# Sample rows' new states formed along the gate and up tiles of the second feed-forward block, readout taken from the old state

## The chip, the core and the metric

One core of a Trainium2 chip runs one launch of the kernel. The metric is the device time of a launch in microseconds (us). Five engines work side by side, each with its own queue in order: TensorE (PE for matmuls, PEld for weight loads), VectorE (DVE), ScalarE (ACT), GpSimd (POOL) and SyncE (SP), which issues the transfers. "L772" is line 772 of the kernel before.

## The reference, cut to what matters

A decoder layer for 512 prompt rows and 8 sample rows (one new token for each of 8 sequences, with its stored state): a half-step SwiGLU block, a mixer of causal pooling and a state-space scan side by side, a second half-step SwiGLU block, and a last norm.

```python
h = h + 0.5 * swiglu(rms_norm(h, ffn1_norm), ...)
h = h + mixer(rms_norm(h, mix_norm), ...)
h = h + 0.5 * swiglu(rms_norm(h, ffn2_norm), ...)   # swiglu: (silu(x @ wg) * (x @ wu)) @ wd
return rms_norm(h, final_norm)
```

For a sample row, head by head, the scan is one step. With the old state h0 (64 x 128 for a head), the head's input x, its step dt, decay = exp(dt * A), and rows B and C of 128 numbers that 8 heads of a group share:

```
new state = decay * h0 + (dt * x) B        (an output, new_ssm_sample)
y         = new state . C + d_skip * x
```

y then goes through the gate with silu(z), a norm by group, and the output projection. The new state itself is needed by nothing else in the launch.

## The kernel before

Activations lie with features on the 128 partitions and the 520 rows (512 prompt, 8 sample, in two halves of 260) along the free axis. Each f32 product is made of three matmuls (`mm3`, L115 to L118): high part of the weights by high and low part of the activations, and low part of the weights by the high part. `split` (L101) makes the parts: ScalarE casts a weight tile to its high part (L106), VectorE subtracts to get the low part (L107).

The feed-forward blocks (`Ffn`) go over 22 tiles of the inner width in chunks of 8, 8 and 6. `rest` (L307) calls `step(f)` for each tile (L329): seven products of 12 matmuls each, copies of partial sums from PSUM (L284), then `gates` (L288: VectorE sums, a Silu on ScalarE in L292) and `close` (L295: the cast of the gated tile L299 and its low part L300). The weights of a tile (`load`, L245) come by two transfers of 512 KB into one of two raw buffers (L249, L250). From them VectorE forms sums (L256 to L258), and ScalarE and VectorE split four tiles: "whi_6a" is the high part of the first weights of tile 6, "shi_6c" and "shi_6d" those of its sums, "whi_6b" the rest. After each chunk, `down` (L339) multiplies the gated tiles with the down weights and adds them to h (L356 to L363); the last chunk does it by halves (`down_by_half`, L378). `scales` (L302) forms the rows' inverse norm (nx[3]) and a second tile rn, which is -0.5 times it (L305), and which the down epilogues L356 and L408 multiply by.

The mixer is written as two plans of stages (CONV_PLAN L38, GATE_PLAN L42): b, x, p and z are the input projections with their convolution or pooling, A and B the two parts of a chunk of the prompt's scan, G and H the gate and norm of a group, o, g and h the output projection, and s2 handles two sample units. A scan part loads a broadcast of decays by SyncE (ab, L796), forms exponentials on ScalarE and products on VectorE (L813, L818, L822), and TensorE multiplies (L831 to L838).

A sample unit is a sequence b and a group g of four 128-row blocks, 16 in all (`sample`, L760). It loads B's and C's rows, broadcast over the partitions (bcb, L764), and the state (h0, 256 KB, L767). For each of four blocks ScalarE makes B times dt*x (L771), VectorE forms decay * h0 plus that, in place (L772); the state is stored (L774), and VectorE multiplies it with C and sums along the row into ysm (L776). `gate` (L877) adds ysm to the sample columns (L884), multiplies with the silu of z (L886), and `gate_out` squares (L895), sums and normalises. The rows B and C of the samples are transposed and sent through a scratch in DRAM by `sample_bc` (L748).

A scheduler places the instructions: it runs through a timeline of its own, with estimated costs, takes on each engine the earliest traced instruction that it holds ready (those in a high-priority block first), and the resulting order of each engine's queue is fixed. `keep_in_program_order` puts an instruction behind the one traced last before it on the same engine. `issue_after(i)` puts a block's instructions that are on i's engine behind i. Tiles with the same tag share a number of buffers; an instruction that writes a reused buffer waits until the earlier tile's readers are done.

## Time and profile before

| what | us |
|---|---|
| three runs | 1028.15, 1032.51, 1027.37 |
| median | 1028.15 |
| profiled execution, its own time | 1030.91 |
| its span | 1029.1 |
| first feed-forward block and start | 0 to about 375 |
| mixer with output projection | about 375 to 633 |
| second feed-forward block to the end | about 633 to 1029.1 |

The span is the time from the first to the last instruction in the profile. An engine is busy while an instruction of its own executes; instructions of one engine overlap a little at their ends, so the distance between the starts of equal neighbours is less than one's duration. In a row of a group stand line, engine, operation, output and input tiles, shape and count, then the busy time and the mean of one, then the idle time in front of them and what ended it. A row of waits reads: who waited for whom, us in total, times, longest. A row of a timeline has start and duration. A row of a stretch has its bounds, its length, the busy time of PE, PEld, DVE, ACT and POOL with counts, the granted clock, the share in which the DMA engines were busy, and GB/s. A row of transfers ends with the median us from issue to landing.

### The profile page before, as it was taken

The page shows a single profiled execution, that of the slowest core. Times are in us where ns is not written, and L with a number is a line of the kernel's source. Part 1 is how long each engine was busy: PE and PEld are TensorE (multiplying, and loading weights), DVE is VectorE, ACT ScalarE, POOL GpSimd, SP SyncE. Part 2 cuts the span into 40 slices and gives each one's busy share as a digit, 9 for nine tenths or more (in the row PEclk, how much of TensorE's full clock was granted, in tenths as well). Part 3 has the DMA queues.
Part 4 walks back from the last instruction along what each step waited for, and adds up shares of the span by engine and source line. Part 5 has one row for each costly group of instructions (what it writes and reads, how often), then busy time and mean ns, then how long its engine had stood idle before and what let it go on. Part 6 is the DMA issues. An engine that isn't in the chain of part 4 may idle for free.

```text
span 1029.1 us, 19313 instructions
## 1 busy us (share of the span) xinstructions
PE 981.7 (95%) x7848; PEld 956.6 (93%) x7848; DVE 807.3 (78%) x1403; ACT 526.4 (51%) x884; POOL 57.0 (6%) x109
## 2 busy tenths in 40 slices
PE   7999999999999999997698999999999999999994
PEld 6999999999999999996598999899999999999994
DVE  7999557995578788689989877999954799557866
ACT  7566314663145555775486525656631566315552
POOL 0000000000000000337201000000000000000000
PEclk9999999999999999999899999999999999999997
DMA  5333223232232143355354222222323323232203
GB/s 186 111 124 123 83 87 119 83 124 82 88 118 93 55 138 116 126 173 183 110 174 145 94 103 82 69 96 91 115 83 103 103 88 119 82 103 104 93 32 83
DMA packets 45352, 110.25 MB, mean 107 GB/s; under 512 B 5896, under 2 KB 17096, under 8 KB 45264
## 3 DMA queue, kind: packets, MB, share of 16 engines
q1 hardware_dynamic: 45264, 109.03, 31.4%
q8 instruction: 61, 1.00, 0.4%
q14 instruction: 27, 0.22, 0.1%
HBM read 101.67 MB, written 7.34 MB: 106 GB/s over the span
## 4 chain that ended last, share of the span: by engine, by line
PE 42%; DVE 7%; ACT 4%; DMA 2%; issue 1%; POOL 1%; DVEq 0%; ACTq 0%; SPq 0%
PE A L116 4%; PE A L117 4%; PE A L118 4%; PE dn L118 3%; PE dn L116 3%; PE dn L117 3%; PE BE L116 3%; PE BE L118 3%; PE BE L117 3%; PE wo L116 2%; PE wo L118 2%; PE wo L117 2%; PE P L228 1%; PE dh L116 1%; DMA bcb<-scr_bc 1%
## 5 line engine op out<-in xcount | busy, mean ns | idle before, releaser
L356 DVE TENSOR_TENSOR td<-dn,rn 128x520 f32<-128x520 f32 x40 | 27.9, 699 | 112.5 <-PE dn L118 112.5
L116 PE MATMUL dn<-g,whi_1d 128*128 128x260 f32 x352 | 99.3, 283 | 1.7 <-ACT whi_1d L106 1.5
L117 PE MATMUL dn<-g,whi_1d 128*128 128x260 f32 x352 | 99.2, 282 | 0.0
L118 PE MATMUL dn<-g,wlo_1d 128*128 128x260 f32 x352 | 99.1, 283 | 0.0
L116 PE MATMUL dn<-g,whi_2d 128*128 128x260 f32 x256 | 72.5, 283 | 1.6 <-ACT whi_2d L106 1.6
L117 PE MATMUL dn<-g,whi_2d 128*128 128x260 f32 x256 | 72.3, 282 | 0.0
L118 PE MATMUL dn<-g,wlo_2d 128*128 128x260 f32 x256 | 72.1, 283 | 0.0
L116 PEld LDWEIGHTS dn<-g,whi_1d 128*128 128x128 f32 x352 | 66.1, 188 | 2.4 <-ACT whi_1d L106 2.0
L284 ACT COPY ac<-A 128x260 f32<-128x260 f32 x123 | 46.0, 375 | 41.3 <-PE A L118 39.7
L117 PEld LDWEIGHTS dn<-g,whi_1d 128*128 128x128 f32 x352 | 66.2, 188 | 0.0
L118 PEld LDWEIGHTS dn<-g,wlo_1d 128*128 128x128 f32 x352 | 66.1, 188 | 0.0
L106 ACT CAST whi_1d<-raw_1d 128x1024 fp32r<-128x1024 f32 (+1 forms) x24 | 23.4, 980 | 70.6 <-PE dn L117 62.2
L228 PE MATMUL P<-xg_f,raw 128*128 128x260 f32 x192 | 46.2, 398 | 5.3 <-DMA raw<-in_w1gu 5.2
L106 ACT CAST whi_2d<-raw_2d 128x1024 fp32r<-128x1024 f32 (+1 forms) x18 | 18.5, 1027 | 63.6 <-PE dn L117 59.2
L116 PEld LDWEIGHTS dn<-g,whi_2d 128*128 128x128 f32 x256 | 48.3, 189 | 2.0 <-ACT whi_2d L106 2.0
L256 DVE TENSOR_TENSOR s<-raw 128x1024 f32<-128x1024 f32 x41 | 49.9, 1217 | 0.0
L117 PEld LDWEIGHTS dn<-g,whi_2d 128*128 128x128 f32 x256 | 48.2, 188 | 0.0
L228 PEld LDWEIGHTS P<-xg_f,raw 128*128 128x128 f32 x192 | 37.5, 199 | 11.5 <-ACT xg_f L178 5.2
L118 PEld LDWEIGHTS dn<-g,wlo_2d 128*128 128x128 f32 x256 | 48.1, 188 | 0.0
L116 PE MATMUL wo<-catg,whi_wo 128*128 128x260 f32 x128 | 37.4, 292 | 0.2 <-DVE h L871 0.2
L116 PE MATMUL inz<-xh_mx,whi_inz 128*128 128x260 f32 x128 | 37.4, 292 | 0.0
L118 PE MATMUL inz<-xh_mx,wlo_inz 128*128 128x260 f32 x128 | 36.9, 288 | 0.0
(1334 smaller groups left out, 3920.3 us busy)
## 6 DMA issues: line engine op xcount, KB each, us to landing
raw<-in_w2gu SPq DMA_DIRECT2D x44, 512.0 KB, 3.7
raw<-in_w1gu SPq DMA_DIRECT2D x42, 512.0 KB, 4.4
raw_1d<-in_w1d SPq DMA_DIRECT2D x16, 512.0 KB, 3.7
raw_2d<-in_w2d SPq DMA_DIRECT2D x16, 512.0 KB, 4.4
raw_wo<-in_w_out SPq DMA_DIRECT2D x12, 512.0 KB, 4.6
h<-in_state_ssm SPq DMA_DIRECT2D x16, 256.0 KB, 4.8
ab<-scr_acs SPq DMA_DIRECT2D x8, 512.0 KB, 5.2
out_nss<-h SPq DMA_DIRECT2D x16, 256.0 KB, 3.3
```

What stands on the lines that cost most here:

```text
L106: nc.scalar.copy(h, src)
L116: nc.tensor.matmul(ps, whi, xhi, start=start, stop=False, **kw)
L117: nc.tensor.matmul(ps, whi, xlo, start=False, stop=False, **kw)
L118: nc.tensor.matmul(ps, wlo, xhi, start=False, stop=stop, **kw)
L228: nc.tensor.matmul(self.banks[f, u][b][:, :HB], ws(self.raw[f][:, u], j + 4 * q), xg[:, slot[q]], start=j == q == 0, stop=j == 3 and q == ...
L256: nc.vector.tensor_tensor(out=s1, in0=diag, in1=up0, op=ALU.add)
L284: nc.scalar.copy(keep, out[:, :HB])
L356: nc.vector.tensor_tensor(out=t, in0=banks[d][:, :, :HB], in1=self.rn.rearrange("p (b t) -> p b t", b=2), op=ALU.mult)
```

## The change

- `sample` loads only C's row and the old state, with buffers for three and four units, and VectorE multiplies the old state with C. The result goes to ysm, the product itself to a tile that nobody reads.
- `sample_bc` also forms, for each sample and group, the sum over B times C, by a small VectorE product and a matmul with ones (sbc). `sample_y`, called in `gate`, makes ysm * decay + (dt * x) * sbc, three VectorE operations for a group.
- `new_states` is a generator that `step` of the second block advances once for each tile from tile 3 on. Its first call loads the first unit; each later call loads the next unit (B's row and the state again) and forms the present one: for each of four blocks ScalarE makes B times dt*x and the scaled state, a transfer on POOL's queue adds the first onto the second in SBUF, and another stores it. Loads and scalings are kept in program order. Two buffers each.
- decay and dt*x (sdec, sxdt) move to a pool that lives on.
- The tile rn goes; the down epilogues multiply by -0.5 and nx[3] in one operation.
- `gate_out` squares whole rows into X, which is no longer needed, where it had squared halves.
- The samples' block under `issue_after` becomes plain.

```diff
@@ -199,6 +199,7 @@
 
         def __init__(self, nx, i, wx, gp, direct):
             self.nx, self.i, self.wx, self.gp, self.direct = nx, i, wx, gp, direct
+            self.states = None
             self.w, self.A, self.BE, self.ac, self.g, self.tg, self.raw, self.banks, self.behind = ({} for _ in range(9))
 
         def plain_load(self, f, j=None):
@@ -301,8 +302,6 @@
 
         def scales(self):
             rstds(self.nx, f"f{self.i}")
-            self.rn = self.wx.tile([P, NT], F32, tag="rn", bufs=1, name=f"rn{self.i}")
-            nc.vector.tensor_scalar(out=self.rn, in0=self.nx[3], scalar1=-0.5, scalar2=None, op0=ALU.mult)
 
         def rest(self, before, last_chunk):
             lo = 0
@@ -327,6 +326,8 @@
                 lo = hi
 
         def step(self, f):
+            if self.states is not None and f > 2:
+                next(self.states, None)
             if f not in self.A:
                 self.product(f, 1)
             if f - 1 not in self.g and f > self.direct:
@@ -353,8 +354,9 @@
             def done(d):
                 t = self.wx.tile([P, 2, HB], F32, tag="tg", bufs=2, name=f"td{self.i}_{d}_{c}")
                 hd = h[:, d].rearrange("p (b t) -> p b t", b=2)
-                nc.vector.tensor_tensor(out=t, in0=banks[d][:, :, :HB], in1=self.rn.rearrange("p (b t) -> p b t", b=2),
-                                        op=ALU.mult)
+                nc.vector.scalar_tensor_tensor(out=t, in0=banks[d][:, :, :HB], scalar=-0.5,
+                                               in1=self.nx[3].rearrange("p (b t) -> p b t", b=2), op0=ALU.mult,
+                                               op1=ALU.mult)
                 if after is None:
                     nc.vector.tensor_tensor(out=hd, in0=t, in1=hd, op=ALU.add)
                     return
@@ -405,7 +407,8 @@
             def done(d, b):
                 hs = HALVES[b]
                 t = self.wx.tile([P, 2, HB], F32, tag="tg", bufs=2, name=f"th{self.i}_{d}{b}")[:, 0]
-                nc.vector.tensor_tensor(out=t, in0=banks[d, b][:, :HB], in1=self.rn[:, hs], op=ALU.mult)
+                nc.vector.scalar_tensor_tensor(out=t, in0=banks[d, b][:, :HB], scalar=-0.5, in1=self.nx[3][:, hs],
+                                               op0=ALU.mult, op1=ALU.mult)
                 nc.vector.tensor_tensor(out=h[:, d, hs], in0=t, in1=h[:, d, hs], op=ALU.add)
                 after(d, b, hs)
 
@@ -491,6 +494,8 @@
     f2["xg"].release()
     xa[0].release()
     g2 = f2["ffn"].gp = pool("g2", "left")
+    f2["st"] = pool("st2", "left")
+    f2["ffn"].states = f2["states"](f2["st"])
     with tc.high_priority():
         f2["ffn"].scales()
         f2["ffn"].behind[2] = f2["ffn"].plain_out(0)
@@ -536,13 +541,14 @@
                 nc.sync.dma_start(out=outs["y"][:, q, t], in_=hg[:, q, t])
 
     f2["ffn"].rest(before2, after2)
-    for p in (ps[0], g2, f2["hg"], f2["wx"]):
+    for p in (ps[0], f2["st"], g2, f2["hg"], f2["wx"]):
         p.release()
 
 
 def mixer(tc, ins, outs, e):
     nc = tc.nc
     cst, act, wp, tmp, dr, pool = (e[x] for x in ("cst", "act", "wp", "tmp", "dr", "pool"))
+    ones = e["ones"]
     bank, load_unit, mm3, ws, v, rstd, rstds, vec, h, nx2, raw_tile, open_f2, fin, fill = (
         e[x] for x in ("bank", "load_unit", "mm3", "ws", "v", "rstd", "rstds", "vec", "h", "nx2", "raw_tile",
                        "open_f2", "fin", "fill"))
@@ -602,7 +608,7 @@
             if not k:
                 nc.tensor.matmul(dtb[b][:NH, :HB], w48[:, k, :NH], xl[:, k, hs], start=False, stop=False)
     rstds(nx2[0], "mx")
-    dv = mp.tile([48, NT], F32, tag="h0", bufs=2, name="dv")
+    dv = mp.tile([48, NT], F32, tag="h0", bufs=4, name="dv")
     for b, hs in enumerate(HALVES):
         nc.vector.tensor_tensor(out=dv[:, hs], in0=dtb[b][:48, :HB], in1=r[:48, hs], op=ALU.mult)
     tok = mp.tile([P, 2, NC + 1, NH], F32, tag="tok", name="tok")
@@ -705,7 +711,7 @@
         first = slice(PAST, PAST + w - 1)
         sx = slice(SAMPLE_P + PAST, LP, 16)
         nc.gpsimd.tensor_tensor(out=cur[:, first], in0=cur[:, first], in1=rcnt[:, : w - 1], op=ALU.mult)
-        held["pool"] = nc.gpsimd.tensor_tensor(out=cur[:, first], in0=cur[:, first], in1=U[:, first], op=ALU.subtract)
+        nc.gpsimd.tensor_tensor(out=cur[:, first], in0=cur[:, first], in1=U[:, first], op=ALU.subtract)
         nc.gpsimd.tensor_copy(npp[:, g], U[:, SEQ : SEQ + PAST])
         nc.gpsimd.tensor_copy(spool[:, g], us[:, :, 1:16])
 
@@ -730,10 +736,15 @@
 
 
     sdt = mp.tile([P, NX, NS], F32, tag="sdt", name="sdt")
-    sdec = mp.tile([P, NX, NS], F32, tag="sdec", name="sdec")
-    sxdt = mp.tile([P, NX, NS], F32, tag="sxdt", name="sxdt")
+    sdec = cst.tile([P, NX, NS], F32, tag="sdec", name="sdec")
+    sxdt = cst.tile([P, NX, NS], F32, tag="sxdt", name="sxdt")
     ysm = mp.tile([P, NX, NS], F32, tag="ysm", name="ysm")
+    sbc = mp.tile([P, 2, NS], F32, tag="sbc", name="sbc")
+    junk = act.tile([P, NT], F32, tag="acc", name="junk")[:, :P]
     scr_bc = dr.tile([NS, 512], F32, name="scr_bc")
+
+    def rows_bc(b, a, g):
+        return scr_bc.rearrange("b (a g n) -> b a g n", a=2, g=2)[b, a, g].unsqueeze(0).to_broadcast([P, P])
 
     def sample_decay():
         for j in range(2):
@@ -749,32 +760,60 @@
         bcs = bank("bcs")
         for j in range(4):
             nc.tensor.transpose(bcs[:NS, j * P : (j + 1) * P], BC[:, j, SEQ:NT], ident)
-        bct = mp.tile([NS, 512], F32, tag="ho", bufs=2, name="bct")
+        bct = mp.tile([NS, 512], F32, tag="h0", bufs=4, name="bct")
         nc.scalar.copy(bct, bcs[:NS, :])
         nc.sync.dma_start(out=scr_bc, in_=bct)
+        dots = bank("dots")[:, : 2 * NS]
+        nc.vector.tensor_tensor(out=sbc, in0=BC[:, 0:2, SEQ:NT], in1=BC[:, 2:4, SEQ:NT], op=ALU.mult)
+        nc.tensor.matmul(dots, ones, sbc.rearrange("p g b -> p (g b)"), start=True, stop=True)
+        nc.scalar.copy(sbc, dots.rearrange("p (g b) -> p g b", g=2))
 
     def sample_x(g):
         gs = slice(4 * g, 4 * g + 4)
         nc.vector.tensor_tensor(out=sxdt[:, gs], in0=sdt[:, gs], in1=X[:, gs, SEQ:NT], op=ALU.mult)
 
+
     def sample(b, g):
+        cb = tmp.tile([P, HB], F32, tag="ta", name=f"cb{b}{g}")[:, :P]
+        nc.sync.dma_start(out=cb, in_=rows_bc(b, 1, g))
+        h0 = mp.tile([P, 4, P], F32, tag="h0", bufs=4, name=f"h0_{b}{g}")
+        nc.sync.dma_start(out=h0, in_=ins["state_ssm"][:, b, 4 * g : 4 * g + 4])
+        for q in range(4):
+            nc.vector.scalar_tensor_tensor(out=junk, in0=h0[:, q], scalar=1.0, in1=cb, op0=ALU.mult, op1=ALU.mult,
+                                           accum_out=ysm[:, 4 * g + q, b : b + 1])
+
+    def sample_y(g):
         gs = slice(4 * g, 4 * g + 4)
-        shp = [P, 4, P]
-        bcb = mp.tile([P, 2, P], F32, tag="bcb", bufs=2, name=f"bcb{b}{g}")
-        nc.sync.dma_start(out=bcb, in_=scr_bc.rearrange("b (a g n) -> b g a n", a=2, g=2)[b, g].unsqueeze(0)
-                          .to_broadcast([P, 2, P]))
-        h0 = mp.tile(shp, F32, tag="h0", bufs=2, name=f"h0_{b}{g}")
-        nc.sync.dma_start(out=h0, in_=ins["state_ssm"][:, b, gs])
-        o = mp.tile(shp, F32, tag="ho", bufs=2, name=f"ho_{b}{g}")
-        for q in range(4):
-            j = 4 * g + q
-            nc.scalar.activation(out=o[:, q], in_=bcb[:, 0], func=AF.Copy, scale=sxdt[:, j, b : b + 1])
-            nc.vector.scalar_tensor_tensor(out=h0[:, q], in0=h0[:, q], scalar=sdec[:, j, b : b + 1], in1=o[:, q],
-                                           op0=ALU.mult, op1=ALU.add)
-        nc.sync.dma_start(out=outs["nss"][:, b, gs], in_=h0)
-        for q in range(4):
-            nc.vector.scalar_tensor_tensor(out=o[:, q], in0=h0[:, q], scalar=1.0, in1=bcb[:, 1], op0=ALU.mult,
-                                           op1=ALU.mult, accum_out=ysm[:, 4 * g + q, b : b + 1])
+        xb = mp.tile([P, 4, NS], F32, tag="xb", name=f"xb{g}")
+        nc.vector.tensor_tensor(out=xb, in0=sxdt[:, gs], in1=sbc[:, g : g + 1].to_broadcast([P, 4, NS]), op=ALU.mult)
+        nc.vector.tensor_tensor(out=ysm[:, gs], in0=ysm[:, gs], in1=sdec[:, gs], op=ALU.mult)
+        nc.vector.tensor_tensor(out=ysm[:, gs], in0=ysm[:, gs], in1=xb, op=ALU.add)
+
+    def new_states(wx):
+        def load(b, g):
+            br = wx.tile([P, P], F32, tag="sb", bufs=2, name=f"br{b}{g}")
+            tc.keep_in_program_order(nc.sync.dma_start(out=br, in_=rows_bc(b, 0, g)))
+            hs = wx.tile([P, 4, P], F32, tag="sh", bufs=2, name=f"hs{b}{g}")
+            tc.keep_in_program_order(nc.sync.dma_start(out=hs, in_=ins["state_ssm"][:, b, 4 * g : 4 * g + 4]))
+            return br, hs
+
+        todo = [(b, g) for g in range(2) for b in range(NS)]
+        ahead = load(*todo[0])
+        for i, (b, g) in enumerate(todo):
+            yield
+            br, hs = ahead
+            if i + 1 < len(todo):
+                ahead = load(*todo[i + 1])
+            o = wx.tile([P, 4, P], F32, tag="so", bufs=2, name=f"so{b}{g}")
+            for q in range(4):
+                j = 4 * g + q
+                for t, u, s in ((o, br, sxdt), (hs, hs[:, q], sdec)):
+                    tc.keep_in_program_order(
+                        nc.scalar.activation(out=t[:, q], in_=u, func=AF.Copy, scale=s[:, j, b : b + 1]))
+            nc.gpsimd.dma_start(out=hs, in_=o, accum_op=ALU.add)
+            nc.gpsimd.dma_start(out=outs["nss"][:, b, 4 * g : 4 * g + 4], in_=hs)
+
+    e["f2"]["states"] = new_states
 
 
     hst = mp.tile([P, 2, 512], F32, tag="hst", name="hst")
@@ -877,6 +916,7 @@
     def gate(g):
         zs = zbox[0]
         gs = slice(4 * g, 4 * g + 4)
+        sample_y(g)
         with tc.issue_after(held["exp"].ins):
             nc.scalar.activation(out=zs[:, gs], in_=zs[:, gs], func=AF.Silu)
         for q in range(4):
@@ -888,12 +928,10 @@
     def gate_out(g):
         zs = zbox[0]
         ry = mp.tile([P, NT], F32, tag="wph", name=f"yr{g}")
-        acc = act.tile([P, NT], F32, tag="acc", name=f"yacc{g}")
+        for q in range(4):
+            nc.scalar.activation(out=X[:, 4 * g + q], in_=zs[:, 4 * g + q], func=AF.Square)
         for b, hs in enumerate(HALVES):
-            sq = [acc[:, hs]] + [tmp.tile([P, HB], F32, tag="ta", name=f"ysq{g}{q}{b}") for q in range(1, 4)]
-            for q in range(4):
-                nc.scalar.activation(out=sq[q], in_=zs[:, 4 * g + q, hs], func=AF.Square)
-            rstd(ry, sq, hs, 512, f"y{g}{b}")
+            rstd(ry, [X[:, 4 * g + q, hs] for q in range(4)], hs, 512, f"y{g}{b}")
         cat = cats[g] = xa.tile([P, 2, 4, NT], F32R, tag="xa", bufs=2, name=f"catg{g}")
         for q in range(4):
             i = 4 * g + q
@@ -908,8 +946,7 @@
     def samples(n):
         for _ in range(n):
             if smp:
-                with tc.issue_after(held["pool"].ins):
-                    sample(*smp.pop(0))
+                sample(*smp.pop(0))
 
     pooled, box = [], {}
 
```

## Prediction

> **What bounds the kernel now.** I read the page's first part, then the busy times by stretch, then TensorE's waits in the weak stretch. All durations below are of the profiled execution; its span is 1029.1 us and its own time 1030.91 us, 2.8 us above the median of 1028.15, so I work out a difference and take it from the median.
>
> ```profile
> PE 981.7 (95%) x7848; PEld 956.6 (93%) x7848; DVE 807.3 (78%) x1403; ACT 526.4 (51%) x884; POOL 57.0 (6%) x109
> ```
> ```profile
> 440.00:570.00 130.00, 110.26 (x876) 101.07 (x876) 120.81 (x359) 84.40 (x190) 42.92 (x58) 0.95 0.48 158
> 570.00:620.00 50.00, 50.00 (x396) 47.96 (x393) 39.44 (x73) 17.78 (x27) 1.24 (x1) 1.00 0.21 77
> 680.00:985.00 305.00, 302.24 (x2499) 300.54 (x2498) 231.37 (x314) 145.11 (x221) 0.00 (x0) 1.00 0.29 101
> ```
> ```profile
> 460.00:510.00 50.00, 36.96 (x267) 32.13 (x265) 49.92 (x134) 29.81 (x68) 25.69 (x34) 0.90 0.45 148
> ```
> Columns: stretch, length, busy PE, PEld, DVE, ACT, POOL, granted clock, DMA share, GB/s. Over the whole span TensorE sets the end. The second feed-forward block (680 to 985 us) has 2.8 us of idle TensorE in 305. The mixer (440 to 570) has 130 - 110.26 = 19.7 us, of which 13.0 lie in 460 to 510, where VectorE is busy 49.92 of 50; there the granted clock also falls to 0.90. Counting clock, TensorE's work in the mixer stretch would fit in 110.26 x 0.95 = 104.7 us: 25 us is the most that a relief of the mixer can give.
>
> ```profile
> PE yd L837 <- DVE ab L822: 7.7, 3, 3.5
> PE pst L834 <- DVE E L848: 6.8, 1, 6.8
> ```
> TensorE waits there for VectorE (total, times, longest): 14.5 of the 19.7 us. So what leaves VectorE's queue in the mixer is worth time; what is added to ScalarE in the second block costs some only if it reaches TensorE.
>
> **The mixer's side.** A sample now loads a state, and four dot products read it; the products with B (L771, ScalarE), the update (L772, VectorE), the store of the state and half of the broadcast row go.
>
> ```profile
> L772 DVE SCALAR_TENSOR_TENSOR h<-h,sdec,ho 128x128 f32<-128x128 f32 x64 | 20.4, 363 | 3.5 <-ACT ho L771 2.2 <-ACT hst L840 1.3
> L776 DVE SCALAR_TENSOR_TENSOR ho<-h,bcb 128x128 f32<-128x128 f32 x64 | 20.0, 347 | 0.0
> L771 ACT ACTIVATE ho<-bcb,sxdt 128x128 f32<-128x128 f32 x64 | 20.4, 389 | 19.0 <-DMA bcb<-scr_bc 17.3 <-DVE wlo_wo L107 1.7
> ```
> ```profile
> 460.00:510.00 50.00, 7.22 (x20) 0.90 0.45 148
> ```
> The first fence is 440 to 573 us (busy, mean ns, then idle before); the second is L772 alone. VectorE loses 20.4 us, ScalarE 20.4 us and an in-order wait of 17.3 us for the row; the 64 dot products (20.0) stay.
> - In 460 to 510 VectorE is full, so its 7.2 us of L772 come off the time one for one. With TensorE fed more evenly I take half of the clock loss back: 36.96 x 0.10 / 2 = 1.8.
> - In 440 to 460 and 510 to 570 TensorE is idle 19.7 - 13.0 = 6.7 us. VectorE's and ScalarE's lateness there comes from L771, L772 and the rows they wait for; I take 4 of the 6.7.
> - Added on VectorE: one product for the B.C sums and three small operations per group for the readout. The nearest row:
>
> ```profile
> L758 DVE TENSOR_TENSOR sxdt<-sdt,X 128x32 f32<-128x32 f32 x1 | 0.2, 192 | 1.3 <-ACT X L674 1.3
> ```
> 7 x 0.2 = 1.4 us, of which I charge 1.0. The added matmul of 16 columns and its copy are charged nothing: TensorE's idle time covers them, at most 0.4 us without it. The 16 half-row squares of L895 become 8 whole-row ones; ScalarE is idle 32 of 50 us in 570 to 620, which hides either form.
> - The queue of SyncE:
>
> ```profile
> SPq L774 <- DVE h L772: 32.6, 6, 12.8
> ```
> The stores behind L772 held SyncE's in-order queue 32.6 us; the weight and decay loads behind them come earlier. State and row now have 4 and 3 buffers. It is the reason why I expect the 4 us above, and no further term. The removed issue order behind the pooling subtract held back only POOL instructions, of which a sample has none: zero.
>
> Mixer: -(7.2 + 1.8 + 4) + 1.0 = **-12.0 us**, bounded by -25 (TensorE's floor) and by -4, if only the second item comes and the rest of the chain stays late.
>
> **The second block's side.** From tile 4 to tile 19, each tile gets eight 128x128 scalings on ScalarE, two loads on SyncE (row, state; one tile ahead), an accumulating SBUF transfer and a store on POOL's queue. The first scaling is pinned behind the preceding Silu, so the eight form a burst. Eight in a row are in the trace, and a tile is this:
>
> ```profile
> 525.77 2.45 ACT L771 ACTIVATE ho<-bcb,sxdt 128x128 f32<-128x128 f32 x8
> ```
> ```profile
> 711.20:721.30 10.10, 10.10 (x86) 10.10 (x85) 9.37 (x14) 6.97 (x12) 0.00 (x0) 1.00 0.29 105
> ```
> ```profile
> 711.26 0.64 ACT L292 ACTIVATE tg<-tg 128x520 f32<-128x520 f32 x1
> 712.26 1.05 ACT L106 CAST whi_6a<-raw 128x1024 fp32r<-128x1024 f32 x1 [0.36 <-PE A L117]
> 713.31 0.63 ACT L299 CAST g<-tg 128x520 fp32r<-128x520 f32 x1
> 714.06 0.38 ACT L284 COPY ac<-A 128x260 f32<-128x260 f32 x1
> ```
> ```profile
> 713.74 1.22 DVE L107 TENSOR_TENSOR wlo_6a<-raw,whi_6a 128x1024 fp32r<-128x1024 f32 x1
> 714.87 0.69 DVE L300 TENSOR_TENSOR g<-tg,g 128x520 fp32r<-128x520 f32 x1
> 716.22 1.23 DVE L107 TENSOR_TENSOR slo_6c<-s,shi_6c 128x1024 fp32r<-128x1024 f32 x1 [0.65 <-ACT shi_6c L106]
> ```
> ```profile
> 716.49 0.28 PE L116 MATMUL A<-xth_f,whi_6a 128*128 128x260 f32 x1
> 718.20 0.28 PE L118 MATMUL A<-xth_f,wlo_6a 128*128 128x260 f32 x1
> ```
> ScalarE: 6.97 + 2.45 = 9.4 of 10.1 us, so it fits by capacity. By position: the Silu ends at 711.9, the burst at 714.35, cast g at 715.0, copy ac at 715.2, cast whi_6a at 716.2. TensorE first needs whi_6a at 716.49 (0.3 us left) and wlo_6a at 718.20; VectorE's subtraction would end at 717.4 (0.8 left). But VectorE, with 10.1 - 9.37 = 0.73 us free, now idles from 713.74 to 715.0 and 715.7 to 716.2, about 1.8 us where it idled 0.65: 1.1 more, 0.4 over its free time. So 0 if the order gives it other work, 0.4 as just counted, and 2.45 - 0.73 = 1.7 if the whole burst passes on to it. I take 0.3, near the counted value. Of the 16 tiles, 9 and 17 follow a down projection, where ScalarE is mostly idle, and their bursts cost nothing: 14 x 0.3 = **+4.2 us**, bounds 0 and 14 x 1.7 = 24.
>
> The waits that this adds:
>
> ```profile
> raw<-in_w2gu SPq DMA_DIRECT2D x44, 512.0 KB, 3.7
> h<-in_state_ssm SPq DMA_DIRECT2D x16, 256.0 KB, 4.8
> out_nss<-h SPq DMA_DIRECT2D x16, 256.0 KB, 3.3
> ```
> ```profile
> 708.58 0.33 SPq L249 DMA_DIRECT2D raw<-in_w2gu  x1
> ```
> ```profile
> 718.57 1.22 DVE L256 TENSOR_TENSOR s<-raw 128x1024 f32<-128x1024 f32 x1
> ```
> A state's load reuses the buffer of two states before and waits on SyncE for that state's store; behind it stand the loads of w2gu. One of these is issued at 708.58, lands some 3.7 us later and is first read at 718.57: 6.3 us spare hide a blocked queue. On ScalarE a burst waits for its state; behind it stand the casts above. The loop is burst, accumulation, store, load, burst over two tiles, 20.2 us. With a POOL issue of 1 us each (an estimate from the 1 to 1.7 us of POOL's operations below), it is 2.45 + A + (1 + 3.3) + 4.8, so it fits while the accumulation A, issue included, is under 8.7 us. No row shows an accumulating transfer; its bounds are a store (3.3) and a load, a read of the target and a store after one another (4.8 + 4.8 + 3.3 = 12.9). I take 4.8 + 1 = 5.8, nearest to the load: hidden. POOL has nothing else to do (0.00 busy in 680 to 985).
>
> **The factor -0.5.** It moves from one operation per block into the down epilogues, which change form:
>
> ```profile
> L305 DVE TENSOR_SCALAR rn<-r_f x2: 418/420/421, 29.7 to 671.4; 128x520 f32<-128x520 f32 x2
> ```
> ```profile
> L239 DVE SCALAR_TENSOR_TENSOR tg<-P,tg x6: 415/418/428, 33.6 to 675.0; 128x260 f32<-128x260 f32 x6
> ```
> ```profile
> L235 DVE TENSOR_TENSOR tg<-P,r_f x6: 366/416/421, 29.1 to 671.7; 128x260 f32<-128x260 f32 x6
> ```
> Both forms from PSUM take 0.42 us, so the epilogues cost the same. Of the two removed operations the one at 671.4 stands between the two evacuations for which the first gate waits: **-0.4 us**.
>
> **Sum:** -12.0 + 4.2 - 0.4 = -8.2, so 1028.15 - 8.2 = 1020.0 us.
>
> **Rivals.**
> 1. The mixer gives little: chain and loads, not VectorE's load, set TensorE's waits. For: the longest single wait (6.8) ends with one operation, E L848; against: VectorE was full ahead of it. Mixer -4, block +4.2, factor -0.4: 1028.
> 2. The burst reaches TensorE through VectorE (slower). It decides once the casts come so late that VectorE idles more than its 0.73 us per tile; with the whole burst, 14 x 1.7 = 24: 1028.15 - 12.4 + 24 = 1040. For: VectorE at 93%; against: the 0.3 and 0.8 us still left above.
> 3. The accumulation takes over 8.7 us. Each tile grows by half the excess: at 12 us 14 x 1.65 = 23, so 1039.
> 4. POOL's descriptor work slows VectorE. In the mixer two copies' residuals took 2.32 us beside POOL's operations and 0.76 without:
>
> ```profile
> 453.26 0.76 DVE L718 TENSOR_TENSOR catp<-PW,catp 128x512 fp32r<-128x512 f32 x2
> 484.12 2.32 DVE L718 TENSOR_TENSOR catp<-PW,catp 128x512 fp32r<-128x512 f32 x2
> ```
> ```profile
> 484.70 1.72 POOL L703 TENSOR_TENSOR PW<-PW 128x652 f32<-128x652 f32 x1
> ```
> If two issues hold VectorE 1 us each per tile, less 0.73 free, 14 x 1.3 = 18 instead of 4.2: 1034. The Trainium skill, "SBUF — State Buffer", section "Who interferes with whom", says that a two-input VectorE operation contends with POOL's reads of SBUF and not with its writes, and infers that descriptor generation needs the write side; by that this rival is nothing. The trace agrees for reads (the pair above); no run here shows descriptors, so its chance is small.
> 5. More than forecast: the mixer falls near TensorE's floor and the bursts hide: -22, so 1006.
> That the work doesn't move as said I rule out: new state times C is the decayed old readout plus the input times B.C, and 19 tiles suffice for 16 states.
>
> **Chances.** Forecast (1012 to 1024) 0.47, rival 1 0.17, rival 2 0.13, rival 3 0.08, rival 4 0.05, rival 5 0.10. A measurement of this kernel can tell about 0.5% from no change, 1023.0 to 1033.3. Faster: 0.47 less 0.03 at its edge, 0.10, and 0.03 of rival 1: 0.57. Same: 0.03, 0.14 and 0.02 of rival 4: 0.19. Slower: the rest of 2 to 4: 0.24. The range of 1007 to 1036 leaves out most of rivals 2 and 3 and the end of 5, under 2 in 10. Most of the chance has one sign.
>
> **What would show it.** Right: TensorE's idle time in the mixer falls from 19.7 to about 8 us and its clock to near 1.0; tiles 4 to 19 take 10.1 to 10.6 us; no ScalarE scaling waits over a microsecond for a state. Wrong: a mixer with VectorE still full; tiles of 11 us or more with VectorE idle behind late casts (rival 2), with ScalarE waiting for DMA (3), or with VectorE's operations stretched (4).

## The result, and the profile after

The changed kernel takes 1027.21 us (median of 20 runs, 1024.12 to 1030.0) beside 1030.42 us for the kernel before (20 runs, 1027.37 to 1032.51): a ratio of 0.9971, 95% interval 0.9962 to 0.998. That is 3.2 us less, within the 0.5% that the prediction called no change, where it had forecast 8.2 us less. The profiled execution took 1027.65 us, its span is 1025.9 us. So the question is where 5 us of the expected gain went.

The page's first line, and then three stretches of the changed kernel (columns as before: stretch, length, PE, PEld, DVE, ACT, POOL, clock, DMA share, GB/s). Line numbers in a row are those of the kernel that the row is from: L292 of the kernel before is L293 of the changed one.

```profile
PE 980.5 (96%) x7850; PEld 957.5 (93%) x7850; DVE 794.5 (77%) x1344; ACT 539.0 (53%) x941; POOL 80.7 (8%) x141
```
```profile
440.00:570.00 130.00, 121.28 (x990) 113.31 (x990) 121.26 (x329) 72.51 (x132) 43.34 (x58) 0.97 0.38 125
460.00:510.00 50.00, 42.09 (x340) 38.56 (x340) 49.93 (x134) 25.61 (x54) 26.04 (x34) 0.93 0.44 145
680.00:985.00 305.00, 296.94 (x2422) 294.55 (x2422) 220.69 (x305) 171.08 (x342) 23.02 (x32) 0.99 0.44 137
```

In the mixer TensorE's idle time fell from 19.7 to 8.7 us and the clock rose from 0.95 to 0.97. In the second block it rose from 2.8 to 8.1 us, and the clock fell from 1.00 to 0.99. The whole page hides both: TensorE is busy within 1.2 us of what it was.

A better reading than busy shares is the clock time at which TensorE begins the same piece of work. I took the first matmul of each product from TensorE's timeline in both traces and subtracted. The differences between neighbouring marks ("psr_f" is the sum of squares of the second block's first norm, "whi_3a" the high part of tile 3's first weights) say where time was won (minus) or lost (plus). Here is the sum for the changed kernel, beside the prediction's terms:

| stretch, by the mark that ends it (start in the kernel before) | after minus before, us | forecast |
|---|---|---|
| start to the second block's normaliser, psr_f (665.51) | -15.22 | -12.0 |
| to tile 3 (whi_3a, 687.90) | -0.67 | -0.4 |
| tiles 3 to 7 (to whi_8a, 736.69) | -0.06 | +1.2 (0.3 for each tile) |
| tiles 8 to 10 (to whi_11a, 817.95) | +1.64 | +0.6 |
| tile 11 (to the second use of whi_12a, 833.79) | +4.06 | +0.3 |
| tiles 12 to 17 (to whi_18a, 933.68) | -0.06 | +1.5 |
| tiles 18 and 19 (to the second use of whi_20a, 962.54) | +3.95 | +0.6 |
| to the first sum of the last norm, psl (1002.32) | +0.02 | 0 |
| the end (to the end of the span) | +3.14 | 0 |
| sum | -3.20 | -8.2 |

The mixer gave more than forecast. The tiles' loss lies in three of these stretches and nowhere else: at tiles 8, 11 and 19. And there is a loss at the end that the prediction did not have at all.

**Tiles 11 and 19.** TensorE's timeline has one wait at each, and ScalarE's timeline shows what it waited for:

```profile
808.81 0.39 PE L116 MATMUL A<-xth_f,shi_11d 128*128 128x260 f32 x1 [1.95 <-ACT ac L285]
```
```profile
800.39 0.63 ACT L293 ACTIVATE tg<-tg 128x520 f32<-128x520 f32 x1
800.93 0.39 ACT L812 ACTIVATE so<-br,sxdt 128x128 f32<-128x128 f32 x1
...
803.78 1.05 ACT L106 CAST shi_11d<-s 128x1024 fp32r<-128x1024 f32 x1
...
805.53 0.64 ACT L293 ACTIVATE tg<-tg 128x520 f32<-128x520 f32 x1
806.07 0.39 ACT L812 ACTIVATE so<-br,sxdt 128x128 f32<-128x128 f32 x1
...
808.12 0.39 ACT L812 ACTIVATE hs<-hs,sdec 128x128 f32<-128x128 f32 x1
808.41 0.35 ACT L285 COPY ac<-A 128x260 f32<-128x260 f32 x1
```

A burst of eight scalings stands behind each Silu. Elsewhere from tile 4 on the Silus are a tile, 9 to 13 us, apart. After a down projection the products of two tiles alternate on TensorE, and the Silus of tiles 9 and 10 are 5.1 us apart, so two bursts of 2.35 us fall into 7.5 us of ScalarE's queue. The kernel before has the same pair, 5.45 us apart:

```profile
814.68 0.63 ACT L292 ACTIVATE tg<-tg 128x520 f32<-128x520 f32 x1
820.13 0.65 ACT L292 ACTIVATE tg<-tg 128x520 f32<-128x520 f32 x1
```

In the changed kernel, behind the second burst stands the copy of a partial sum out of bank A (L285), and TensorE may not write its next product into A before that. The operand shi_11d had been ready since 804.8.

A wait of 1.95 us and a loss of 4.06: most of the rest is the clock. Stretches of 2 us from the start of that wait:

```profile
807.00:809.00 2.00, 0.19 (x1) 0.19 (x2) 2.00 (x5) 2.00 (x9) 0.77 (x2) 1.00 0.94 338
809.00:811.00 2.00, 2.00 (x13) 2.00 (x13) 1.32 (x2) 1.51 (x3) 0.66 (x1) 0.69 0.97 316
811.00:813.00 2.00, 2.00 (x12) 2.00 (x11) 0.85 (x2) 0.38 (x1) 0.00 (x0) 0.50 0.61 121
813.00:815.00 2.00, 2.00 (x18) 2.00 (x18) 0.53 (x1) 1.22 (x2) 0.57 (x1) 0.95 0.51 169
```

After the wait TensorE is busy without a gap, but the granted clock is 0.69, 0.50 and 0.95, which is 2 x (0.31 + 0.50 + 0.05) = 1.7 us of lost work. 1.95 + 1.7 = 3.7 of the 4.06. Busy time does not show it; the clock column and the count of matmuls (12 in 2 us, where 19 is full) do.

The clock does not always fall behind this wait. In a trace of another kernel (e4_tail_order, below) TensorE waits the same 1.95 us at the same matmul, and the clock stays at 1.00:

```profile
809.96 0.39 PE L116 MATMUL A<-xth_f,shi_11d 128*128 128x260 f32 x1 [1.95 <-ACT ac L285]
```
```profile
812.00:814.00 2.00, 2.00 (x19) 2.00 (x18) 1.00 (x2) 1.05 (x2) 0.00 (x0) 1.00 0.76 161
```

There the same tile loses 2.57 us. What tells the two apart is said in the last section.

**Tile 8.** Here VectorE waited for weights, and TensorE for VectorE's low part (slo_8d):

```profile
725.44 1.23 DVE L257 TENSOR_TENSOR s<-raw 128x1024 f32<-128x1024 f32 x1 [2.56 <-DMA raw<-in_w2gu]
```
```profile
728.47 0.39 PE L118 MATMUL A<-xth_f,slo_8d 128*128 128x260 f32 x1 [1.34 <-DVE slo_8d L107]
```
```profile
716.72 0.33 SPq L797 DMA_DIRECT2D hs<-in_state_ssm  x1
717.57 0.42 SPq L251 DMA_DIRECT2D raw<-in_w2gu  x1
```
```profile
SPq L797 <- DMA out_nss<-hs: 90.8, 12, 9.9
```

The last row is SyncE's wait in 680 to 985 us: a state's load waits for the store of the state two before, 12 times, up to 9.9 us, and the weights' loads stand behind it in the queue. L257 reads the second half of the weights, which L251 loads. That load was issued at 717.57, 5.3 us before VectorE was free for L257 (725.44 - 2.56 = 722.88), and took 7.8 us to land. In the kernel before, the same half was issued at 729.15, 9.6 us before its read at 738.77, and took 4.7 us. So it came both later and slower. The clock stayed at 1.00 after this shorter wait of TensorE, so it cost 1.64.

**The end.** ScalarE's rows of the square root for the first half of the last norm, before and after:

```profile
1000.60 1.28 ACT L528 ACT_TABLE_LOAD   x1
1002.96 0.48 ACT L528 ACTIVATE r_last<-psl,eps 128x260 f32<-128x260 f32 x1 [1.08 <-PE psl L525]
```
```profile
1008.20 1.28 ACT L533 ACT_TABLE_LOAD   x1
1009.49 0.48 ACT L533 ACTIVATE r_last<-psl,eps 128x260 f32<-128x260 f32 x1
1009.87 0.41 ACT L517 ACTIVATE sq_last<-h 128x260 f32<-128x260 f32 x1
1011.07 0.48 ACT L533 ACTIVATE r_last<-psl,eps 128x260 f32<-128x260 f32 x1 [0.80 <-PE psl L532]
```

In each pair the first row loads ScalarE's table for the square root. Before, the square root ran 26 us ahead of the end of the span, beside the second half's matmuls. After, its sum (psl) was also early, at 995.98 us, but the square root waited until 1009.49, 16 us ahead of the end; table load, square root, reciprocals and products of the first half now queue up with those of the second.

### The profile page after: what moved, and what is told of

Its sections match the earlier page's. It is cut to its first block, busy times and chain, and to the rows that moved or that the text cites. A ratio compares the mean times of both kernels' runs of the same rounds, so it can differ in the third digit from the quotient of the medians.

```text
span 1025.9 us, 19405 instructions
## 1 busy us (share of the span) xinstructions
PE 980.5 (96%) x7850; PEld 957.5 (93%) x7850; DVE 794.5 (77%) x1344; ACT 539.0 (53%) x941; POOL 80.7 (8%) x141
## 4 chain that ended last, share of the span: by engine, by line
PE 85%; DVE 6%; ACT 4%; DMA 2%; issue 1%; POOL 0%; SPq 0%; DVEq 0%; ACTq 0%; POOLq 0%
PE A L116 7%; PE A L117 7%; PE dn L116 7%; PE dn L118 7%; PE A L118 7%; PE dn L117 7%; PE BE L116 6%; PE BE L117 6%; PE BE L118 6%; PE P L229 4%; PE wo L116 2%; PE wo L118 2%; PE wo L117 2%; PE inz L116 1%; PE inz L118 1%
## 5 line engine op out<-in xcount | busy, mean ns | idle before, releaser
L357 DVE SCALAR_TENSOR_TENSOR td<-dn,r_f 128x520 f32<-128x520 f32 x40 | 27.9, 699 | 112.8 <-PE dn L118 112.8
L285 ACT COPY ac<-A 128x260 f32<-128x260 f32 x123 | 45.8, 373 | 33.4 <-PE A L118 32.6
L257 DVE TENSOR_TENSOR s<-raw 128x1024 f32<-128x1024 f32 x41 | 50.0, 1220 | 2.6 <-DMA raw<-in_w2gu 2.6
L106 ACT CAST whi_2d<-raw_2d 128x1024 fp32r<-128x1024 f32 (+1 forms) x18 | 18.5, 1028 | 63.1 <-PE dn L117 59.3
L117 PE MATMUL inz<-xl_mx,whi_inz 128*128 128x260 f32 x128 | 36.6, 286 | 0.0
```

The lines of the kernel that those rows point to most:

```text
L106: nc.scalar.copy(h, src)
L117: nc.tensor.matmul(ps, whi, xlo, start=False, stop=False, **kw)
L257: nc.vector.tensor_tensor(out=s1, in0=diag, in1=up0, op=ALU.add)
L285: nc.scalar.copy(keep, out[:, :HB])
L357: nc.vector.scalar_tensor_tensor(out=t, in0=banks[d][:, :, :HB], scalar=-0.5, in1=self.nx[3].rearrange("p (b t) -> p b t", b=2), op0=ALU.mult,
```

## The experiments

My theory after this reading: (a) the mixer's gain comes from VectorE's load; (b) tiles 11 and 19 are lost to ScalarE's double bursts, tile 8 to transfers; (c) the end is lost to the edit of the factor -0.5, through the order of the work. Rivals are named in each expectation. For each run the same table of marks was made; it is given for all of them after the first group. All ratios are to the kernel before, measured beside the run.

### The mixer alone, and the tiles' losses one by one

Run e1_mixer_only, the new states left out:

```diff
-    f2["ffn"].states = f2["states"](f2["st"])
```

> Leaves out the sample rows' new states (that output is not written); all else is the changed kernel. My theory: the mixer gains 15 us, the second block's tiles lose 9 us through the states, and the end loses 4 us through another cause. So the tiles 8, 11 and 19 lose nothing here, the first normaliser of the second block still comes at about 652 us, the end still has the late square root, and the time is 9 us under the changed kernel: about 1018 us (0.988 of the kernel before). Rival: the late end comes from the states' transfers on POOL's queue; then the end is as before too and the time is about 1013 us.

Measured: 1020.61 us, ratio 0.9896 (0.9878 to 0.9915).

Run e8_no_add_store, loads and scalings kept:

```diff
-            nc.gpsimd.dma_start(out=hs, in_=o, accum_op=ALU.add)
-            nc.gpsimd.dma_start(out=outs["nss"][:, b, 4 * g : 4 * g + 4], in_=hs)
```

> Leaves out the adding transfer and the store of each new state (that output is not written); loads and the eight scalings stay. My theory: the losses at tiles 11 and 19 stay (3.9 us each), that at tile 8 goes: 1 to 2 us less than the changed kernel, about 1025.5 us. Rival (transfers): all of the 9 us go, about 1018 us.

Measured: 1026.91 us, ratio 0.9954 (0.9937 to 0.9972).

Run e3_three_buffers, `bufs=3` for "sb" and "sh" in `new_states`:

> Three buffers in place of two for the states' loads and rows, so that a load no longer waits for the store of two states before. My theory: only the late weights at tile 9 come from it, so 1.6 us less than the changed kernel, about 1025.5 us, and SyncE's wait for that store (90.8 us in all) goes mostly. Rival (transfers): the whole loss of the tiles comes from SyncE held by stores, so 8 to 9 us less, about 1018 us.

Measured: 1028.92 us, ratio 0.9978 (0.9969 to 0.9988).

Run e2_skip_10_18:

```diff
-            if self.states is not None and f > 2:
+            if self.states is not None and f > 2 and f not in (10, 18):
```

> No state is formed at tiles 10 and 18; the later ones move back, to tile 21. My theory: the two bursts of scalings within 5 us at the start of a chunk delay ScalarE's copies of partial sums, for which TensorE waits, and its clock falls after that; without it tiles 11 and 19 lose nothing, 7 to 8 us less than the changed kernel: about 1019.5 us. Rival (transfers): the loads and stores that hold SyncE are as many as before, so the time stays within 2 us of the changed kernel, 1025 to 1028 us.

Measured: 1024.32 us, ratio 0.9932 (0.9913 to 0.9952).

The marks, us after minus before, one profiled execution each (runs further down included; "end" from the first sum of the last norm). The stretches left out are within 0.1 of the first table's, but for +0.4 in tiles 3 to 7 of e15 and before the last norm of e2, e12 and e17:

| kernel | to normaliser | tiles 8-10 | tile 11 | 12-17 | 18-19 | end | all |
|---|---|---|---|---|---|---|---|
| the change | -15.22 | +1.64 | +4.06 | -0.06 | +3.95 | +3.14 | -3.2 |
| e1_mixer_only | -12.76 | -0.08 | +0.03 | -0.13 | +0.03 | +3.77 | -9.9 |
| e8_no_add_store | -14.83 | -0.06 | +4.05 | -0.09 | +3.97 | +3.79 | -3.9 |
| e3_three_buffers | -13.82 | +1.17 | +2.55 | -0.06 | +3.94 | +3.85 | -3.1 |
| e2_skip_10_18 | -14.66 | +1.26 | +0.02 | +4.50 | +0.02 | +3.71 | -5.5 |
| e4_tail_order | -13.63 | +1.21 | +2.57 | -0.09 | +2.44 | +5.02 | -3.2 |
| e5_factor_only | +0.15 | -0.06 | +0.03 | -0.11 | +0.03 | +4.43 | +3.7 |
| e11_own_buffer | -13.52 | +0.96 | +4.06 | -0.10 | +3.95 | -0.30 | -5.7 |
| e13_factor_own | +0.11 | -0.07 | +0.03 | -0.11 | +0.02 | -1.13 | -1.9 |
| e12_own_skip_3buf | -13.43 | +1.08 | +0.03 | +4.20 | +0.03 | +0.14 | -8.3 |
| e17_skip_pool_loads | -13.03 | -0.04 | +0.03 | -0.08 | +0.03 | +0.44 | -13.0 |
| e15_own_halves | -13.81 | -0.04 | +4.08 | +0.91 | +0.03 | +1.07 | -8.0 |
| e14_own_halves_3buf | -13.88 | +1.16 | +0.03 | -0.09 | +0.03 | +0.02 | -13.5 |
| e16_halves_pool_loads | -14.12 | -0.06 | +0.51 | +0.88 | +0.02 | -0.48 | -14.0 |

The four runs split the tiles' loss. Without the states no tile loses anything (e1). Without addition and store tile 8's loss is gone, and tiles 11 and 19 keep theirs to 0.02 us (e8), so these are not the transfers' doing. Without the first of the two close bursts they are gone too (e2). The table also gives the noise of the first column: twelve kernels with the same mixer code, all but e5 and e13, won 12.8 to 15.2 us there, in one execution each; a mixer figure finer than that is not to be had from one trace.

Where the loss at tiles 11 and 19 stands behind whole bursts, it is 2.4 to 2.6 us or 3.9 to 4.1 us behind the same wait of 1.95 us: the larger where the clock fell, the smaller where it did not (e3 at tile 11, e4 at both). The edits of e3 and e4 do not touch this wait, so part of the changed kernel's 4.06 and 3.95 is chance of the one execution.

Two things did not go by theory. The third buffer left 1.17 of tile 8's 1.64 us, and SyncE's wait for stores fell only from 90.8 us in 12 waits to 64.8 in 9. And in e2 a new loss of 4.5 us stood at tiles 14 to 16. Both came back to the transfers, below.

### What in the mixer made the gain

Run e6_dve_back gives VectorE the removed 64 operations back (behind each dot product, into the tile that nobody reads), with no load and no store:

```diff
+            nc.vector.scalar_tensor_tensor(out=junk, in0=h0[:, q], scalar=sdec[:, 4 * g + q, b : b + 1], in1=cb,
+                                           op0=ALU.mult, op1=ALU.add)
```

> The changed kernel with one more operation of L772's form on VectorE beside each dot product, its result unused. If VectorE's load made the mixer's 15 us, the second block's first normaliser comes 10 to 16 us later than at 652 us; if ScalarE's part, SyncE's stores or the rows' buffers made it, less than 4 us later.

Run e7_act_back gives ScalarE its 64 products back, into a tile of their own:

```diff
+            nc.scalar.activation(out=idle, in_=cb, func=AF.Copy, scale=sxdt[:, 4 * g + q, b : b + 1])
```

> The changed kernel with one scaling of L771's form on ScalarE beside each dot product, its result unused; it waits for the row as L771 did. If VectorE's load made the mixer's gain, that normaliser comes less than 4 us later than at 652 us; if ScalarE's in-order wait for the row made it, 8 us or more.

Measured, one execution each: 1040.69 us, the normaliser only 1.37 us earlier than in the kernel before; and 1031.17 us, the normaliser 12.31 us earlier. Against the twelve traces' 12.8 to 15.2, VectorE's operations are worth 11.4 to 13.9 us, nearly the whole gain, and ScalarE's 0.5 to 2.9, hardly more than the spread of that column. This shows that the gain needs VectorE's relief; whether that alone would have been enough is not shown, since no run takes only these operations away and keeps the stores. But the place differs from what the prediction thought. In e6 the output projection still begins 12 us early; the loss comes later, in one wait of TensorE in 555 to 655 us:

```profile
PE psr_y L160 <- ACT X L934: 8.4, 1, 8.4
```
```profile
L784 DVE SCALAR_TENSOR_TENSOR junk<-h,sdec,cb x64: 255/348/1254, 444.5 to 605.5; 128x128 f32<-128x128 f32 x64
```

With nothing pinning them, the sample units drifted back, the last to 605.5 us, and their readouts made a gate's squares late. I read this so: the scheduler moves work to where VectorE has room, and what counts is VectorE's sum over the mixer and the output projection, not over the 50 us where it looks full. In the changed kernel VectorE is just as full there (49.93 of 50) as before, with work that came forward from later.

### The end

Run e5_factor_only is the kernel before with the new epilogues alone and no rn:

> The kernel before with the factor -0.5 moved into the down epilogues, and nothing else. My theory: this edit alone moves the late square root to the end; 0.4 to 0.7 us gained at the second block's start, 4.4 us lost at the end: 3 to 4 us over the kernel before, about 1033.5 us. Rival, as I predicted: 0.4 us less, and the end's loss belongs to the states or the mixer: about 1029.5 us.

Measured: 1035.66 us, ratio 1.0039 (1.0026 to 1.0052). The edit that removes two operations costs 4 us by itself.

Run e4_tail_order held back the second half's squares behind the first half's square root on ScalarE, since I took the scheduler's order for the cause:

```diff
+        with tc.issue_after(root[0].ins) if b and d else nullcontext():
             sumsq(last, d, hs, f"l{d}{b}")
```

> ScalarE's last squares of the second half are queued behind the square root of the first half, as the order was before. My theory: the changed kernel's end is 4.4 us longer because that square root, with its table load, comes after all squares; so 4 us less than the changed kernel, about 1023 us. Rival: the end is longer for another reason (transfers on POOL's queue at the end), and the time stays within 1 us of 1027.

Measured: 1028.52 us, ratio 0.9978 (0.9963 to 0.9993); the end lost 5.02 us in place of 3.14. The theory fell, and the row of the square root says why:

```profile
1005.21 0.48 ACT L534 ACTIVATE r_last<-psl,eps 128x260 f32<-128x260 f32 x1 [11.57 <-DVE th L410]
```

It now stood early in the queue and waited 11.57 us for VectorE's epilogues. `r_last` and `r_f` (nx[3]) have the same tag, "r", and the pool "act" has one buffer for a tag: the last norm's factor lies in the place of the second block's. Before, the epilogues read rn and the place was free from the last gate on. With rn gone they read r_f up to the last one, and the new tile may not be written until they are done. The new theory needs only a place of its own for r_last:

```diff
-    rl = act.tile([P, NT], F32, tag="r", name="r_last")
...
         res.append(f2["hg"].tile([P, KD, NT], F32, tag="hg", name="hg"))
+        res.append(f2["hg"].tile([P, NT], F32, tag="rl", name="r_last"))
...
-        hs, hg = HALVES[b], res[0]
+        hs, (hg, rl) = HALVES[b], res
```

Run e11_own_buffer, the changed kernel with this:

> The changed kernel, with a buffer of its own for r_last (the square root at the end), which until now takes the place of r_f, the factor that the down epilogues read. New theory: without rn the last epilogue reads r_f, so the first half's square root, its table load, its reciprocal and its products must wait for it; that is the 4.4 us from the last TensorE group to the end. Then here the first half's square root starts near where the kernel before has it (some 15 us before the end), the stretch from the last group to the end falls from 15.6 to about 11.2 us, and the time is about 4.4 us under the changed kernel's, near 1022.8. Rival: the two-factor form of the epilogue itself is slower at the end; then nothing changes, 1027.

Run e13_factor_own, e5_factor_only with this:

> The kernel before with the factor edit alone (the run of that edit gave a ratio of 1.0039) and r_last in its own buffer. Theory (shared buffer): the 4.4 us at the end go and the edit's small gain is left, about 1.2 us under the kernel before, ratio 0.999. Rival (the epilogue's form): the ratio stays at 1.004.

Measured: 1022.4 us, ratio 0.9924 (0.9909 to 0.9939), and 1029.24 us, ratio 0.9991 (0.9977 to 1.0006). In e11 the square root is back:

```profile
997.56 0.48 ACT L533 ACTIVATE r_last<-psl,eps 128x260 f32<-128x260 f32 x1 [1.09 <-PE psl L530]
```

Against the same kernels with the shared place the ratio falls by 0.0047 and 0.0048, some 4.9 us both times, with the epilogue's form unchanged. The shared buffer is the cause, and no cost of the form is left to see (e13's interval includes 1), as the prediction had it.

### Placing the states so that nothing is lost

Run e12_own_skip_3buf joins e11, e3 and e2:

> The changed kernel with r_last in its own buffer, no state at tiles 10 and 18 (the states move back by a tile each, the last at tile 21), and three buffers for row and state. Theory: the double bursts at tiles 10 and 11, and 18 and 19, cost 3.9 us each, the late square root 4.4, and the loss near tile 15 in the run that only left out tiles 10 and 18 was a w2gu load late behind a state's load that had waited for a store. If the third buffer cures that, what is left is tile 8: about 1027.2 - 3.9 - 3.9 - 4.4 = 1015, and up to 1016.5. Rival: the transfers' amount, not the wait for the buffer, makes w2gu late; then tile 15 or another loses its 4.5 us again, 1019.5.

Run e14_own_halves_3buf joins e11 and e3 and cuts each burst in two, four scalings at the start of a tile and four after its fourth product:

```diff
             for p in (2, 5, 6, 3, 7) if f == KF - 1 else (5, 6, 3, 7, 2):
                 self.product(f, p)
+                if p == 6 and self.states is not None and f > 2:
+                    next(self.states, None)
...
             for q in range(4):
+                if q == 2:
+                    yield
                 j = 4 * g + q
```

> The changed kernel with r_last in its own buffer, three buffers for row and state, and each burst of eight scalings cut in two halves of four: one at the start of the tile, one after its fourth product (p = 6). All 16 states at tiles 4 to 19 as in the change. Theory: a burst costs at tiles 11 and 19 because 2.35 us in one piece, twice within 5 us, make the copy ac late; halves of 1.2 us fit, so the 3.9 us at each of them fall to under 1, and the time is near that of the run that leaves out tiles 10 and 18, about 1016. Rival: ScalarE's total work in these two tiles is too much wherever it lies; then 3 to 4 us stay at each, 1023.

Measured: e12 1019.78 us, ratio 0.9901 (0.9885 to 0.9918), the rival's number; e14 1016.09 us, ratio **0.9859 (0.9843 to 0.9876)**, faster than both kernels. In e14 tiles 11 and 19 lose nothing, and what is left of TensorE's waits for ScalarE's copies in 680 to 985 us is short (the first row is the changed kernel's, the second e14's):

```profile
PE A L116 <- ACT ac L285: 4.4, 4, 2.0
```
```profile
PE A L116 <- ACT ac L285: 0.5, 2, 0.2
```

So it was the burst in one piece and at that place, not ScalarE's total; e3, with the third buffer and whole bursts, still loses at both tiles. The loss at tile 15 stayed in e12, third buffer or not:

```profile
848.46 1.23 DVE L257 TENSOR_TENSOR s<-raw 128x1024 f32<-128x1024 f32 x1 [2.90 <-DMA raw<-in_w2gu]
```
```profile
840.91 0.33 SPq L797 DMA_DIRECT2D hs<-in_state_ssm  x1
841.79 0.42 SPq L251 DMA_DIRECT2D raw<-in_w2gu  x1
...
848.66 0.33 SPq L797 DMA_DIRECT2D hs<-in_state_ssm  x1
```

That left two readings: the states' loads block SyncE's queue (in e12 they still waited for stores, 74.6 us in 9 waits), or the transfers slow each other. Two of three further runs decide. The edit of e16 (on e14) and e17 (on e12) moves the states' loads to POOL's queue and leaves their amount as it is:

```diff
-            tc.keep_in_program_order(nc.sync.dma_start(out=hs, in_=ins["state_ssm"][:, b, 4 * g : 4 * g + 4]))
+            tc.keep_in_program_order(nc.gpsimd.dma_start(out=hs, in_=ins["state_ssm"][:, b, 4 * g : 4 * g + 4]))
```

> The version that leaves out tiles 10 and 18 with whole bursts, three buffers and r_last in its own buffer (ratio 0.9901, 4.2 us lost at tiles 14 to 16 where VectorE waits for a w2gu load), with the states' loads on POOL's queue. Theory (the blocked queue): the loss at tiles 14 to 16 goes, ratio 0.986. Rival (the transfers together): it stays, 0.990.

> The fastest version so far (ratio 0.9859) with the states' loads of the second block issued on POOL's queue in place of SyncE's; rows and weights stay on SyncE. Theory (the blocked queue): SyncE no longer waits for the stores, the w2gu loads go out as early as in the kernel before, tile 8's 1.1 us go, and the ratio is 0.985. Rival (the transfers together): the w2gu loads go out early and land late; tile 8 keeps its 1.1 us, 0.986.

Run e15 is e14 with two buffers:

> The fastest version so far (r_last in its own buffer, bursts in halves, three buffers for row and state; ratio 0.9859) with two buffers as in the change. Theory: the halves alone take away the losses at tiles 11 and 19, and the third buffer does little, as in the run of that edit alone: ratio 0.986 to 0.988, with tile 8 at 1.1 to 1.6 us. Rival: the halves need the third buffer; then tiles 8 to 19 lose 3 us or more, ratio 0.989 or above.

Measured: e17 1017.14 us, ratio 0.9859 (0.9845 to 0.9874), and the losses at tiles 8 and 15 are gone; in its trace VectorE starts the same sum without a wait:

```profile
843.69 1.22 DVE L257 TENSOR_TENSOR s<-raw 128x1024 f32<-128x1024 f32 x1
```

Its load went out well ahead:

```profile
834.84 0.44 SPq L251 DMA_DIRECT2D raw<-in_w2gu  x1
```

That is 8.9 us before the sum, and it took 5.7 us to land; in e12 it went out 3.8 us before VectorE was free for the sum, and took 6.5. At tile 8 of e17 the load takes 7.8 us, as in the changed kernel, but is issued 8.9 us ahead in place of 5.3, and no wait is left. So it was the blocked queue that made the losses; slower transfers alone did not. In e16 tile 8's loss went as well, but 1.4 us came at tiles 11 to 13; its ratio, 0.9868 (0.9852 to 0.9885), can't be told from e14's. e15 took 1022.4 us, ratio 0.9907 (0.9893 to 0.9922): there my expectation failed and the rival held. With halves and two buffers ScalarE itself waits for a state, and everything behind it is late:

```profile
815.43 0.40 ACT L816 ACTIVATE hs<-hs,sdec 128x128 f32<-128x128 f32 x1 [3.62 <-DMA hs<-in_state_ssm]
```
```profile
817.67 0.39 PE L116 MATMUL A<-xth_f,whi_11b 128*128 128x260 f32 x1 [2.10 <-ACT ac L285]
```
```profile
820.00:822.00 2.00, 2.00 (x9) 2.00 (x10) 2.00 (x4) 0.81 (x1) 0.77 (x1) 0.50 0.71 194
```

Again a wait of two us, again the clock at 0.50 behind it, and 4.08 us lost.

## Why the prediction was wrong, and where it was right

- **The mixer, -12.0: right in kind, a little small.** It won 12.8 to 15.2 us over twelve traces. The item "in 440 to 460 and 510 to 570 ... I take 4 of the 6.7" was the small one: by the first use of the z weights (whi_inz, 500.76 us in the kernel before) 7.35 us were won, and another 7.43 from there to the start of the output projection. VectorE's operations are the cause (e6); ScalarE's relief, which the prediction had also counted as part of the chain, gave hardly more than the spread between traces (e7). The sign "a mixer with VectorE still full" was badly chosen: it is still full, and the gain is there.
- **"14 x 0.3 = +4.2" failed as a step.** The loss is 9.6 us, at three tiles (1.64, 4.06 and 3.95). The working followed the burst into the casts and on to VectorE, of a tile in mid-chunk, and there it was right: tiles 4 to 7 and 12 to 17 lost nothing. Of the tiles behind a down projection it said only that 9 and 17 cost nothing; right behind them the Silus crowd, and the bursts with them. The trace of before showed that pair of Silus. Nor did it ask what else stands behind the burst: the copy that frees a PSUM bank for TensorE directly, and not by way of VectorE, as rival 2 had it. And it priced a wait at its own length; where the clock falls behind it, the loss is twice that.
- **"6.3 us spare hide a blocked queue" failed.** The wait on SyncE that it described came, 12 times. The spare time was also misread: the sum at 718.57 reads the second half (L250, issued at 708.95, landed at 713.46), so 5.1 us were spare. At tile 8 the blocked queue took 4.3 of them and the slower transfer 3.1 more: 1.64 us lost (e8 and e17).
- **"So the epilogues cost the same": right for the operation, wrong for the edit.** A term put at zero came to +3.1 in the profile, 4.9 by the ratios of e11 and e13. The step that failed asked only how long each form takes. It did not ask who needs the place that the new operand keeps alive.
- **-0.4 at the block's start** came as -0.67.
- **The measured time lies beside rival 1's 1028 us by coincidence.** Rival 1 had the mixer give 4 us; it gave 12.8 or more, and other losses used it up. The profiled execution of the changed kernel has both the largest mixer gain of the twelve and the lowered clock at both tiles, so its single terms carry some chance; their sum, -3.2, is also the difference of the medians.
- **The accumulation** was put at 5.8 us with the limit 8.7. Its transfer took 5.1 us from issue to landing, and 8.1 at its slowest, under the limit; none of the changed kernel's scalings waited for its state (the last number, idle time, is zero). Rival 3 did not occur.

```profile
hs<-so POOLq DMA_DIRECT2D x16, 256.0 KB, 5.1
```
```profile
L812 ACT ACTIVATE hs<-hs,sdec 128x128 f32<-128x128 f32 x64 | 24.9, 389 | 0.0
```

- **Rival 4, POOL's descriptors, did not occur.** VectorE's rows beside such an issue have their usual durations (1.22 us for L257 and 0.69 for L292; the same forms take 1.22 and 0.69 us in the kernel before, where POOL issues nothing there):

```profile
803.66 0.86 POOL L813 DMA_DIRECT2D hs<-so  x1 [13.81 <-ACT hs L812]
```
```profile
802.94 1.22 DVE L257 TENSOR_TENSOR s<-raw 128x1024 f32<-128x1024 f32 x1
804.08 0.69 DVE L292 TENSOR_TENSOR tg<-tg,r_f 128x520 f32<-128x520 f32 x1
```

What the prediction quoted for it from the Trainium skill, "SBUF — State Buffer", section "Who interferes with whom" (two-input VectorE operations don't contend with descriptor generation, which the page marks as inferred), agrees with these rows.

## What to carry to other kernels

When an edit lets an instruction read another tile, look up what shares that tile's buffer: the price is paid by the next writer of the place, here one square root at the very end. A burst that fits on average must be placed where the engine's queue is most crowded, tile by tile, and followed to the first instruction that frees something for the bounding engine; cutting it in halves, with a third buffer, took the loss away. A load that waits for a store does not belong in the in-order queue that feeds the bounding engine.

## What the runs showed of the hardware

- A wait of TensorE can cost about twice its length, or not, by where it falls. In every trace here the clock is lowered only in stretches that begin whole multiples of 3.41 us apart and, but for the last one of a trace, which runs past its end, last 3.41 us or a multiple of it; the changed kernel's second block has two, 39 steps apart:

```profile
809.77:813.18 3.41, 3.41 (x18) 3.41 (x17) 1.84 (x2) 1.11 (x3) 0.00 (x0) 0.50 0.72 183
942.89:946.30 3.41, 3.41 (x19) 3.41 (x17) 1.71 (x2) 1.16 (x3) 0.29 (x1) 0.50 0.49 94
```

- Between 640 and 990 us the traces hold 14 waits of 1.95 to 1.97 us. Behind 9 of them the clock was 0.50 for 3.41 us, and the stretch lost 3.9 to 4.1 us; behind 5 (e3 at tile 11, e4 and e6 at both tiles) it stayed at 1.00, and the stretch lost 2.4 to 2.6. Laid on the steps of 3.41 us of its own trace, each of the 9 has 1.88 us or more inside one step, each of the 5 at most 1.74. Waits of 2.10 (e15), 2.76 (e12) and 2.82 us (e2), with 2.03 or more inside one step, lowered it; waits of 1.34 to 1.58 did not. The Trainium skill, "TensorE: Matmul & The Clock Gate", section "Why this matters for your kernels", asks for no idle gap over about 3 us; here gaps of two thirds of that lowered the clock in 9 of 14 cases.
- An accumulating transfer of 256 KB from SBUF onto SBUF landed in 5.1 us (median of 16; 3.3 to 8.1) and took 0.87 us of POOL to issue (mean); a plain store of the same size 2.3 and 0.57 us.
